# Layer 1's MLP: its norm's scale taken inside the first four chunks, their inputs split anew, and the residual turned without TensorE

## The chip, the cores and the metric

One NeuronCore of one Trainium2 chip runs the whole program. The metric is device time in microseconds (us), the median of several executions. Engines are named as the profile names them: PE is TensorE (PEld its weight loads), DVE is VectorE, ACT is ScalarE, POOL is GpSimd, SP is SyncE, which here only issues DMAs. Each engine works through its own queue of instructions in order; an instruction whose inputs are not there yet holds up all that stands behind it on the same engine.

## The reference, cut to what matters

512 tokens, 1024 channels, two layers. Layer 0 mixes by pooling, layer 1 by attention; each is followed by a gated MLP with a causal convolution of width 3 over the tokens.

```python
def rms_norm(x, g):
    return x * lax.rsqrt(jnp.mean(x * x, axis=-1, keepdims=True) + 1e-6) * g

def conv_glu_ffn(h, w_in, conv_w, conv_b, w_out):
    u = h @ w_in                                   # 512x1024 @ 1024x5632
    c = causal_depthwise_conv(u, conv_w) + conv_b  # 3 taps along the tokens
    a, g = c[..., :2816], c[..., 2816:]
    return (a * silu(g)) @ w_out                   # 2816 -> 1024

for i in range(2):
    h = h + mixer[i](rms_norm(h, norm_mix[i]))
    h = h + conv_glu_ffn(rms_norm(h, norm_ffn[i]), ...)
return rms_norm(h, norm_f)
```

The change is in the last MLP, that of layer 1.

## The kernel before, in words

**Arithmetic.** Every large product runs as three fast matmuls: an operand is split into a high part (a rounded copy, made by ACT) and a low part (the remainder, made by DVE), and `mm3` adds high x high (L89), high weight x low input (L90) and low weight x high input (L91) into one PSUM bank. A weight tile of 128x1024 thus costs one DMA from SP, one ACT copy (L103) and one DVE subtraction (L106). Three raw tiles, four high and four low tiles rotate.

**Layout.** Activations lie with channels on the partitions, `h[0..7]`, each 128x512 (two neighbours share one tile `hp[e]`). The inputs of the MLP, `f1x_h` and `f1x_l`, are the split of h times the norm's gain g; the norm's per-token factor r is not in them. At the end of attention, each `h[m]` gets its residual (L1232), is split (L244 makes `f1x_l`), and its squares are added to `n_acc`, by POOL (L220).

**Up-projection, `mlp_in`.** 44 chunks of 128 hidden channels, in the order gate 0, value 0, gate 1, value 1 and so on (`wi_0_1`, `wi_0_0`, `wi_1_1`, ...; the second number is 1 for the gate). A chunk is 8 k-steps of three matmuls, 24 matmuls into one bank. The first four chunks go together, k outermost: at each k, three matmuls for each of four banks. The bank ring is 5, 0, 1, 2, 3, 4. Call E the end of these 96 matmuls. Behind them comes the norm's statistics: a DVE reduction of `n_acc` (L225), a small matmul (L226), and 1/sqrt by three Newton steps in thirteen small DVE instructions (L186 to L200); ACT and DVE spread the result over all partitions as `n_rb` (L234, L236). Then, for each of the 44 chunks, `conv_chunk` multiplies the bank by `n_rb` into a buffer u (L681, DVE), ACT makes the first tap with the bias (L684), and DVE adds the other two (L685, L686). ACT applies silu to the gate (L724) and DVE multiplies (L733) and makes sums of halves for a later product with fewer multiplications (L738 to L761).

**Residual turned, `turned`.** The end of the kernel wants h with tokens on the partitions. PE transposes it by 32 matmuls with the identity (L792), eight sets of four into banks 6 and 7, and ACT copies each set out (L793, x8) into `ht`. A set is issued behind each of the eight chunks after the first group.

**Tokens and down-projection.** After 22 chunks, `mlp_tokens` multiplies by the down weights (`wt_...`, tiles a11, a12, a22 and their sums; some sums are formed by a second DMA that adds into the first one's tile, issued by POOL at L811), then the remaining chunks, another `mlp_tokens`, and an end part.

**Order.** A scheduler at build time orders each engine's instructions by its estimate of when they can run; `pin` keeps an instruction in the order of the source, and `tc.issue_after(x)` keeps what is inside behind x.

Of the kernel before, what the change touches and what calls it, by code (L numbers as in the profile page):

```python
# [37 lines left out]
NF = FF // P  # L38
# [24 lines left out]
def trunk(ctx: ExitStack, tc: tile.TileContext, x_tok, x_t, vecs, w_pool, w_kq, w_v, w_o, gain, w_in, w_half, w_down, w_end, w_tok, out):  # L63
    nc = tc.nc
    V, A, G, T = nc.vector, nc.scalar, nc.gpsimd, nc.tensor
# [46 lines left out]
    def in_weights(layer, j, s, eng=None, raw=None, pin=lambda ins: ins):  # L112
        return weights(w_in[layer][j, s], D, f"wi{layer}_{j}_{s}", eng, raw, 256 if eng else 1024, pin)

    pin = tc.keep_in_program_order
    eps = small(cst, 1, 32, name="eps")
    V.memset(eps, EPS)

    def load_root(x, name):

        A.activation(small(sm, 1, 32, tag="root", name=name), x, AF.Sqrt)

    load_root(eps, "root0")

# [30 lines left out]
    for g, w in enumerate(WINDOWS):  # L155
        b = band[:, g, :]
# [45 lines left out]
    class Norm:  # L202
# [5 lines left out]

        def square(self, c, lo, hi, sq=None):
            sq = sq or sm.tile([P, S], F32, tag="sq", name=f"{self.name}_sq{c}_{lo}")  # L210
            A.activation(sq[:, lo:hi], h[c][:, lo:hi], AF.Square)  # L211
# [19 lines left out]
        def spread(self, r):  # L231

            wide = sm.tile([P, S], F32, tag="sq", name=f"{self.name}_wide")
            A.activation(wide.rearrange("p (b i) -> p b i", i=SQ), r.unsqueeze(2).to_broadcast([P, NB, SQ]), AF.Copy)  # L234
            rb = sm.tile([P, S], F32, tag="rb", name=f"{self.name}_rb", bufs=1)
            V.transpose(rb, wide)  # L236
            return rb
# [124 lines left out]
    def mlp_halves(fp, xs, norm, ws0, after):  # L362
# [312 lines left out]
        for x in fills:  # L675
            pass

    def conv_chunk(fp, layer, ps, rb, m, name):

        u = fp.tile([P, S], F32, tag="u", name=f"{name}_u", bufs=3)  # L680
        V.tensor_tensor(u, ps, rb, ALU.mult)  # L681
        cw = [col(V_CW + (layer * 3 + t) * 2 * NF + m) for t in range(3)]
        t = fp.tile([P, S], F32, tag="t", name=f"{name}_t", bufs=4)
        A.activation(t, u, AF.Identity, bias=col(V_CB + layer * 2 * NF + m), scale=cw[2])  # L684
        V.scalar_tensor_tensor(t[:, 1:], u[:, : S - 1], cw[1], t[:, 1:], ALU.mult, ALU.add)  # L685
        V.scalar_tensor_tensor(t[:, 2:], u[:, : S - 2], cw[0], t[:, 2:], ALU.mult, ALU.add)  # L686
        return t

    def mlp_in(fp, layer, xs, norm, ws0, z, turns):

        pairs = [k for n, k in GROUPS for _ in range(n)]
        todo = [(j, s) for j in range(NF) for s in (1, 0)]
        together = 4 if ws0 is None else 2
        groups = [todo[i : i + together] for i in range(0, 4, together)] + [[t] for t in todo[4:]]
        conv, pend, r, rb, y = [None, None], [], None, None, None
        def load(group):
            return [ws0.pop(0) if ws0 else in_weights(layer, j, s) for j, s in group]

        stops, first = set(), 0
        for n, sums in GROUPS:  # L700
            first += 2 * n
            stops.add(min(first - 1 + sums, NF - 1))
        ahead = load(groups[0])
        for i, group in enumerate(groups):
            ws, ahead = ahead or load(group), None
            pss = [bank("ps") for j, s in group]
            for k in range(NC):
                for w, ps in zip(ws, pss):
                    mm3(ps, part(w, k), xs[k], k == 0, k == NC - 1)
# [4 lines left out]
            if rb is None:
                if len(pend) < 4:
                    continue
                if r is None:
                    r = norm.stats(bank("aux"))
                    continue
                rb = norm.spread(r)  # L720
            for (j, s), ps in pend:
                conv[s] = conv_chunk(fp, layer, ps, rb, s * NF + j, f"c{layer}_{j}_{s}")
                if s == 1:
                    A.activation(conv[1], conv[1], AF.Silu)  # L724
# [8 lines left out]
                V.tensor_tensor(o, conv[0], conv[1], ALU.mult)  # L733
                if pairs[e]:
                    if not odd:
                        split_sum(y, z[e], 0, 0, 1, -1.0 if layer else 1.0)
                    elif layer:
                        V.tensor_tensor(y[:, 4:6, :], y[:, 0:2, :], y[:, 1:4:2, :], ALU.subtract)  # L738
                        V.tensor_tensor(y[:, 6, :], y[:, 4, :], y[:, 3, :], ALU.add)
# [9 lines left out]
                if s == 0:  # L749
                    yield j  # L750
            pend = []
            next(turns, None)
# [17 lines left out]
    def mlp(fp, xs, norm):  # L770

        z, ht = [], []
        up = mlp_in(fp, 1, xs, norm, None, z, turned(fp, ht))
        done, first = 0, 0
        for g, (n, sums) in enumerate(GROUPS):
            upto = first + 2 * n
            while done < min(upto + sums, NF):
                done = next(up) + 1
            zg = z[first // 2 : upto // 2]
            if sums:  # L780
                mlp_tokens(g, zg, ht)
            first = upto
        return plain(zg), ht

    def turned(fp, ht):

        for j in range(NT):
            ht.append(fp.tile([P, D], F32, tag="ht", name=f"ht{j}", bufs=NT))
            for a in range(2):
                ps = bank("aux")  # L790
                for c in range(4):
                    T.transpose(ps[:, c * P : (c + 1) * P], h[4 * a + c][:, j * P : (j + 1) * P], ident)  # L792
# [173 lines left out]
    norm0, norm1, norm2 = (Norm(f"n{i}") for i in range(3))  # L966
# [7 lines left out]
    ws0 = []  # L974
# [7 lines left out]
    with tc.tile_pool(name="ap", bufs=2) as ap:  # L982
# [56 lines left out]
        for c in range(2):  # L1039
            u = ap.tile([P, S], F32, name=f"ku{c}", bufs=1)  # L1040
# [92 lines left out]
        todo = work()  # L1133
# [191 lines left out]
```

## Time and profile before

| | |
|---|---|
| median of 3 runs | 899.01 us (898.3 to 900.18) |
| profiled execution, its own time | 897.72 us |
| its span (first to last instruction) | 895.9 us |
| mean granted PE clock | 0.996 |
| busy: PE, PEld, DVE, ACT, POOL | 884.4, 765.6, 698.0, 475.6, 247.6 us |
| first group of four up chunks starts | 535.00 us |
| first token matmul | 637.02 us |

Times in the trace count from the start of the span. A row of the timeline gives start, length, engine, line, operation, output and inputs, a count, and in brackets how long the engine stood idle before it and what released it. A row of the groups gives the count, the busy sum and the mean of one in ns. Matmuls and DVE instructions overlap their neighbours, so their pace is the distance between starts, not their length.

### The profile page before, as it was taken

To read this page: it belongs to the slowest core of one execution; us is meant where nothing else is said; L and a number is where in the kernel's file an instruction comes from. 1 tells how busy PE (TensorE), PEld (TensorE's weight loads), DVE (VectorE), ACT (ScalarE), POOL (GpSimd) and SP (SyncE) were. 2 spreads that over 40 slices of the span, in tenths; PEclk is the share of its full clock that TensorE was granted. 3 is DMA by queue.
4 is the path that set the end of the run, shared out by engine and by line. 5 is a ranking of instruction groups with operands and counts; after the bars stand their busy time and mean duration, and the time that the engine had idled before them with its cause. 6 is when DMAs were issued, how large, how long until landed. Compare 5 with 4: busy or idle time off the path is not lost.

```text
span 895.9 us, 12904 instructions
## 1 busy us (share of the span) xinstructions
PE 884.4 (99%) x4770; PEld 765.6 (85%) x4770; DVE 698.0 (78%) x1110; ACT 475.6 (53%) x776; POOL 247.6 (28%) x327
## 2 busy tenths in 40 slices
PE   9999999999999999999999999999999999999996
PEld 8888889999999998898888888888888888888885
DVE  7899998878787876665887472999977888967744
ACT  7756655555464643546887451754534443434434
POOL 4867332313122300427665030001230002300004
PEclk9999999999999999999999999999999999999998
DMA  9444255565656443122110041175384231452202
GB/s 332 140 131 131 93 162 151 150 186 141 165 142 162 122 129 83 60 94 94 48 48 25 24 159 54 71 235 140 72 243 156 96 98 42 94 188 94 94 24 94
DMA packets 37118, 106.82 MB, mean 119 GB/s; under 512 B 3904, under 2 KB 5952, under 8 KB 37056
## 3 DMA queue, kind: packets, MB, share of 16 engines
q1 hardware_dynamic: 33600, 93.69, 31.8%
q0 software_dynamic: 3312, 12.06, 7.8%
q8 instruction: 37, 0.61, 0.3%
q10 hardware_dynamic: 144, 0.26, 0.1%
q14 instruction: 25, 0.20, 0.1%
HBM read 103.90 MB, written 2.10 MB: 118 GB/s over the span
## 4 chain that ended last, share of the span: by engine, by line
PE 89%; DVE 8%; ACT 1%; issue 1%; POOL 0%; ACTq 0%; DVEq 0%
PE bank L89 28%; PE bank L90 28%; PE bank L91 28%; PE bank L1157 1%; PE bank L1185 1%; DVE bank L393 1%; PE bank L288 1%; DVE tl L412 1%; DVE uw_hold_l L468 1%; PE bank L255 1%; DVE a_t L374 1%; ACT sc L1173 0%; DVE a_t L359 0%; DVE ty L420 0%; DVE g_t L358 0%
## 5 line engine op out<-in xcount | busy, mean ns | idle before, releaser
L89 PE MATMUL bank<-f1x_h,wi_h 128*128 128x512 f32 x352 | 137.7, 391 | 0.0
L90 PE MATMUL bank<-f1x_l,wi_h 128*128 128x512 f32 x352 | 137.0, 389 | 0.0
L91 PE MATMUL bank<-f1x_h,wi_l 128*128 128x512 f32 x352 | 136.8, 390 | 0.0
L103 ACT ACTIVATE wi_h<-wi_raw 128x1024 fp32r<-128x1024 f32 x58 | 61.3, 1060 | 86.5 <-PE bank L90 67.3
L91 PEld LDWEIGHTS bank<-f1x_h,wi_l 128*128 128x128 f32 x352 | 66.1, 188 | 13.9
L89 PEld LDWEIGHTS bank<-f1x_h,wi_h 128*128 128x128 f32 x352 | 66.1, 188 | 13.5
L90 PEld LDWEIGHTS bank<-f1x_l,wi_h 128*128 128x128 f32 x352 | 66.1, 188 | 13.5
L106 DVE TENSOR_TENSOR wi_l<-wi_raw,wi_h 128x1024 fp32r<-128x1024 f32 x44 | 53.8, 1225 | 27.0 <-ACT wi_h L103 27.0
L485 POOL TENSOR_TENSOR uw_r_raw<-uw_r_raw,uw_u_raw 128x512 f32<-128x512 f32 x15 | 25.0, 1668 | 161.7 <-DVE uw_hold_l L468 149.0
L106 POOL TENSOR_TENSOR wi_l<-wi_raw,wi_h 128x256 fp32r<-128x256 f32 x56 | 54.0, 994 | 27.3 <-ACT wi_h L103 27.3
L91 PE MATMUL bank<-th,uw_hold_l 128*128 128x256 f32 x180 | 50.9, 283 | 0.0
L90 PE MATMUL bank<-tl,uw_hold_h 128*128 128x256 f32 x180 | 50.9, 283 | 0.0
L89 PE MATMUL bank<-th,uw_hold_h 128*128 128x256 f32 x180 | 50.8, 282 | 0.0
L681 DVE TENSOR_TENSOR c_u<-bank,n_rb 128x512 f32<-128x512 f32 x44 | 30.1, 688 | 22.2 <-PE bank L91 22.0
L220 POOL TENSOR_TENSOR n_acc<-n_acc,n_sq 128x512 f32<-128x512 f32 x14 | 20.4, 1457 | 90.8 <-ACT n_sq L211 90.7
L90 PE MATMUL bank<-f0x_l,wi_h 128*128 128x512 f32 x112 | 43.6, 389 | 0.0
L91 PE MATMUL bank<-f0x_h,wi_l 128*128 128x512 f32 x112 | 43.6, 389 | 0.0
L89 PE MATMUL bank<-f0x_h,wi_h 128*128 128x512 f32 x112 | 43.0, 390 | 0.0
L531 DVE TENSOR_TENSOR h<-bank,h 128x512 f32<-128x512 f32 x48 | 32.9, 686 | 11.8 <-PE bank L91 11.4
L467 ACT ACTIVATE uw_hold_h<-wo_raw 128x512 fp32r<-128x512 f32 (+1 forms) x48 | 28.4, 591 | 25.7 <-PE bank L90 18.8
L686 DVE SCALAR_TENSOR_TENSOR c_t<-c_u,vec,c_t 128x510 f32<-128x510 f32 x44 | 40.9, 932 | 1.2
L823 POOL TENSOR_TENSOR wt_a_raw<-wt_a_raw,wt_s_raw 128x1024 f32<-128x1024 f32 x4 | 11.3, 2835 | 102.5 <-DVE wt_a_l L106 102.5
(437 smaller groups left out, 2771.6 us busy)
## 6 DMA issues: line engine op xcount, KB each, us to landing
wi_raw<-w_in SPq DMA_DIRECT2D x58, 512.0 KB, 3.3
wo_raw<-w_down SPq DMA_DIRECT2D x32, 256.0 KB, 2.7
uw_u_raw<-w_half SPq DMA_DIRECT2D x15, 512.0 KB, 5.5
uw_u_raw<-w_half POOLq DMA_DIRECT2D x15, 512.0 KB, 5.6
uw_r_raw<-w_half SPq DMA_DIRECT2D x15, 512.0 KB, 3.5
wt_a_raw<-w_tok SPq DMA_DIRECT2D x12, 512.0 KB, 3.8
kq_raw<-w_kq SPq DMA_DIRECT2D x10, 512.0 KB, 3.3
wo_raw<-w_o SPq DMA_DIRECT2D x8, 512.0 KB, 3.3
```

Source lines behind the costliest of these rows:

```text
L89: T.matmul(ps, lhsT=wh, rhs=xh, start=start, stop=False, **kw)
L90: T.matmul(ps, lhsT=wh, rhs=xl, start=False, stop=False, **kw)
L91: T.matmul(ps, lhsT=wl, rhs=xh, start=False, stop=stop, **kw)
L103: pin(A.activation(h[:, :n], raw[:, :n], AF.Copy))
L106: (eng or V).tensor_tensor(l[:, o], raw[:, o], h[:, o].bitcast(F32), ALU.subtract)
L220: eng.tensor_tensor(self.acc[:, lo:hi], self.acc[:, lo:hi], sq[:, lo:hi], ALU.add)
L467: A.activation(w[0], raw, AF.Copy)
L485: G.tensor_tensor(r[:, :n], r[:, :n], u[:, n:], ALU.add)
L531: V.tensor_tensor(h[m], ps, h[m], ALU.add)
L681: V.tensor_tensor(u, ps, rb, ALU.mult)
L686: V.scalar_tensor_tensor(t[:, 2:], u[:, : S - 2], cw[0], t[:, 2:], ALU.mult, ALU.add)
L823: G.tensor_tensor(r[:, :n], r[:, :n], raws["s1", s][:, :n], ALU.add)
```

## The change

Six edits, all around layer 1's MLP:

1. The statistics move into the first group, ahead of its third k-step, with 1/sqrt by ACT's square root (its table loaded during attention), a DVE reciprocal and one Newton step. The last addition into `n_acc` is DVE's instead of POOL's.
2. While the first group still runs, `rescale(k)` makes h times g times r for each of the eight inputs (DVE L708, into a buffer `xs_k`), then splits it anew into the same tiles: ACT L709 `f1x_h`, DVE L709 `f1x_l`. Both overwrite the inputs that the first group reads, so that each waits for the group's last matmul on that input.
3. The next chunk's weights (`wi_2_1`) are split between the fifth and the sixth of these, kept in the source's order.
4. Only the first four banks are still multiplied by `n_rb`, in place (L683), and not before the last rescaled input. The 40 later chunks go from PSUM straight to the taps (ACT L686, DVE L687, L688); their L681 is gone.
5. The next weights of the chunks after the first group are loaded as before in the source (`ahead = load(...)`).
6. The 32 PE transposes and eight ACT copies are gone. Four DVE transposes of 128x1024 (L813, within blocks of 32x32, all into one buffer `turn`) and 64 ACT copies of 32 partitions x 256 (L818) put h into `ht`: 16 copies beside the statistics, two behind each chunk's first tap, one behind each silu, the rest ahead of the tokens.

```diff
-        u = fp.tile([P, S], F32, tag="u", name=f"{name}_u", bufs=3)
-        V.tensor_tensor(u, ps, rb, ALU.mult)
+        if rb is not None:
+            V.tensor_tensor(ps, ps, rb, ALU.mult)
...
-        A.activation(t, u, AF.Identity, bias=col(V_CB + layer * 2 * NF + m), scale=cw[2])
...
+        taps.append(A.activation(t, ps, AF.Identity, bias=col(V_CB + layer * 2 * NF + m), scale=cw[2]))
+        V.scalar_tensor_tensor(t[:, 1:], ps[:, : S - 1], cw[1], t[:, 1:], ALU.mult, ALU.add)
+        V.scalar_tensor_tensor(t[:, 2:], ps[:, : S - 2], cw[0], t[:, 2:], ALU.mult, ALU.add)
...
+        def turn(n, ins):
+            with tc.issue_after(ins.ins):
+                for x in range(n):
+                    next(turns, None)
+
+        def rescale(k):
+            y = fp.tile([P, S], F32, tag="t", name=f"xs{layer}_{k}", bufs=4)
+            V.scalar_tensor_tensor(y, h[k], col(V_NFF + layer * NC + k), rb, ALU.mult, ALU.mult)
+            return pin(A.activation(xs[k][0], y, AF.Copy)), V.tensor_tensor(xs[k][1], y, xs[k][0].bitcast(F32), ALU.subtract)
...
             for k in range(NC):
+                if i == 0 and k == 2:
+                    r = norm.stats(bank("aux"), root=True)
+                    turn(12, norm.last)
+                    rb = norm.spread(r)
+                    turn(4, norm.wide)
                 for w, ps in zip(ws, pss):
                     mm3(ps, part(w, k), xs[k], k == 0, k == NC - 1)
...
+            if i == 0:
+                for k in range(NC):
+                    if k == 5:
+                        ahead = load(groups[1], pin)
+                    behind = rescale(k)
...
-            for (j, s), ps in pend:
-                conv[s] = conv_chunk(fp, layer, ps, rb, s * NF + j, f"c{layer}_{j}_{s}")
+            for (j, s), ps in zip(group, pss):
+                with ExitStack() as order:
+                    for x in () if i else behind:
+                        order.enter_context(tc.issue_after(x.ins))
+                    conv[s] = conv_chunk(fp, layer, ps, None if i else rb, s * NF + j, f"c{layer}_{j}_{s}")
+                if i:
+                    turn(2, taps[-1])
...
-                for c in range(4):
-                    T.transpose(ps[:, c * P : (c + 1) * P], h[4 * a + c][:, j * P : (j + 1) * P], ident)
-                A.activation(ht[j][:, a * S : (a + 1) * S], ps, AF.Copy)
...
+            V.transpose(x, hp[e])
...
+                    A.activation(
+                        whole[dst, :, 2 * e : 2 * e + 2, src].rearrange("p j c i -> p c j i"),
+                        x[src, :, :, q, :],
+                        AF.Copy,
+                    )
...
-            norm2.add(m)
+            norm2.add(m, eng=V if m == NC - 1 else G)
+            if m == NC // 2:
+                pin(load_root(eps, "root2"))
```

The instructions on DVE around the end of the first group. Before, this is the piece from the statistics' reduction on; the four `wi` splits are those of chunks 4, 5 and 6:

```order
L225 TENSOR_REDUCE n_part<-n_acc 128x16
L106 TENSOR_TENSOR wi_2_1_l<-wi_2_1_raw,wi_2_1_h 128x1024
L106 TENSOR_TENSOR wi_2_0_l<-wi_2_0_raw,wi_2_0_h 128x1024
L186 TENSOR_SCALAR rs_v<-bank_76 128x16
L106 TENSOR_TENSOR wi_3_1_l<-wi_3_1_raw,wi_3_1_h 128x1024
L188 TENSOR_SCALAR rs_i<-rs_v 128x16
```

The low part of chunk 6's weights, `wi_3_1_l`, is there the third split, ahead of the Newton steps and of everything that the convolutions do.

In the changed kernel the same queue goes from chunk 4's weights through the last rescaled inputs into the multiplications of the first four banks (bank 5 is `bank_75`, bank 0 `bank_70`):

```order
L106 TENSOR_TENSOR wi_2_1_l<-wi_2_1_raw,wi_2_1_h 128x1024
L709 TENSOR_TENSOR f1x_l<-xs_5_5801,f1x_h 128x512
L709 TENSOR_TENSOR f1x_l<-xs_6_5805,f1x_h 128x512
L106 TENSOR_TENSOR wi_2_0_l<-wi_2_0_raw,wi_2_0_h 128x1024
L709 TENSOR_TENSOR f1x_l<-xs_7_5809,f1x_h 128x512
L683 TENSOR_TENSOR bank_75<-bank_75,n_rb 128x512
L683 TENSOR_TENSOR bank_70<-bank_70,n_rb 128x512
L683 TENSOR_TENSOR bank_71<-bank_71,n_rb 128x512
L683 TENSOR_TENSOR bank_72<-bank_72,n_rb 128x512
L687 SCALAR_TENSOR_TENSOR c_0_1_t<-bank_75,vec,c_0_1_t 128x511
```

Six more tap instructions follow, on banks 5, 0, 1 and 2, and then this piece, on the first pair's products and chunk 4's taps (bank 3), which ends with the weights of chunk 6:

```order
L754 TENSOR_TENSOR y_0_5824<-c_0_0_t,c_0_1_t 128x512
L688 SCALAR_TENSOR_TENSOR c_1_0_t<-bank_72,vec,c_1_0_t 128x510
L779 SCALAR_TENSOR_TENSOR zl_0_5826<-y_0_5824,zh_0_5825 128x256
L754 TENSOR_TENSOR y_0_5824<-c_1_0_t,c_1_1_t 128x512
L687 SCALAR_TENSOR_TENSOR c_2_1_t<-bank_73,vec,c_2_1_t 128x511
L759 TENSOR_TENSOR y_0_5824<-y_0_5824 128x512
L688 SCALAR_TENSOR_TENSOR c_2_1_t<-bank_73,vec,c_2_1_t 128x510
L760 TENSOR_TENSOR y_0_5824<-y_0_5824 128x256
L106 TENSOR_TENSOR wi_3_1_l<-wi_3_1_raw,wi_3_1_h 128x1024
L761 TENSOR_TENSOR y_0_5824<-y_0_5824 128x256
```

`wi_3_1_l` is still the third split, but no longer right behind the second: the last rescaled input, the four banks, their taps and the first products have moved ahead of it. From `wi_2_1_l` to it, both counted, there are now 25.

On PE, before, at the start of chunk 6 (bank 5 for the second time), two transposes of a set stand ahead of its plain rows of three:

```order
L792 MATMUL bank_76<-ident,h_98 128x128 x2
L792 MATMUL bank_76<-ident,h_99 128x128 x2
L89 MATMUL bank_75<-f1x_h,wi_3_1_h 128x512
L90 MATMUL bank_75<-f1x_l,wi_3_1_h 128x512
L91 MATMUL bank_75<-f1x_h,wi_3_1_l 128x512
L89 MATMUL bank_75<-f1x_h,wi_3_1_h 128x512
```

In the changed kernel, at the same place:

```order
L91 MATMUL bank_74<-f1x_h,wi_2_0_l 128x512
L89 MATMUL bank_75<-f1x_h,wi_3_1_h 128x512
L90 MATMUL bank_75<-f1x_l,wi_3_1_h 128x512
L89 MATMUL bank_70<-f1x_h,wi_3_0_h 128x512
L90 MATMUL bank_70<-f1x_l,wi_3_0_h 128x512
L89 MATMUL bank_71<-f1x_h,wi_4_1_h 128x512
L90 MATMUL bank_71<-f1x_l,wi_4_1_h 128x512
L91 MATMUL bank_75<-f1x_h,wi_3_1_l 128x512
L89 MATMUL bank_75<-f1x_h,wi_3_1_h 128x512
```

The transposes are gone, and the first two matmuls of chunks 7 and 8 have moved ahead of chunk 6's first use of `wi_3_1_l`.

On SP, the DMAs ahead of the first token stage (`wt_0` and `wt_1` are its two sets of weights; a `wt_s` tile gets its second half from POOL's adding DMA, and its sum with the `a` tile is one more weight). Before:

```order
L95 DMA wi_8_0_raw<-w_in 128x1024
L817 DMA wt_1_a_raw<-w_tok 128x1024
L810 DMA wt_1_s_raw<-w_tok 128x1024
L817 DMA wt_0_a_raw<-w_tok 128x1024
L817 DMA wt_1_a_raw<-w_tok 128x1024
L817 DMA wt_0_a_raw<-w_tok 128x1024
L810 DMA wt_0_s_raw<-w_tok 128x1024
```

In the changed kernel:

```order
L95 DMA wi_8_0_raw<-w_in 128x1024
L846 DMA wt_1_a_raw<-w_tok 128x1024
L846 DMA wt_0_a_raw<-w_tok 128x1024
L846 DMA wt_1_a_raw<-w_tok 128x1024
L846 DMA wt_0_a_raw<-w_tok 128x1024
L839 DMA wt_1_s_raw<-w_tok 128x1024
L839 DMA wt_0_s_raw<-w_tok 128x1024
```

The first `wt_1_s` has moved behind three `wt_a` transfers, and now waits for the split of the first `wt_0_s` on DVE, where before it waited for a matmul only.

More of the change, by code (lines that the diff above doesn't have):

```diff
@@ L119, in load_root @@
     def load_root(x, name):
-        A.activation(small(sm, 1, 32, tag="root", name=name), x, AF.Sqrt)
+        return A.activation(small(sm, 1, 32, tag="root", name=name), x, AF.Sqrt)
     load_root(eps, "root0")
@@ L210, in square @@
             sq = sq or sm.tile([P, S], F32, tag="sq", name=f"{self.name}_sq{c}_{lo}")
-            A.activation(sq[:, lo:hi], h[c][:, lo:hi], AF.Square)
+            self.last = A.activation(sq[:, lo:hi], h[c][:, lo:hi], AF.Square)
             return sq
@@ L233, in spread @@
             wide = sm.tile([P, S], F32, tag="sq", name=f"{self.name}_wide")
-            A.activation(wide.rearrange("p (b i) -> p b i", i=SQ), r.unsqueeze(2).to_broadcast([P, NB, SQ]), AF.Copy)
+            self.wide = A.activation(wide.rearrange("p (b i) -> p b i", i=SQ), r.unsqueeze(2).to_broadcast([P, NB, SQ]), AF.Copy)
             rb = sm.tile([P, S], F32, tag="rb", name=f"{self.name}_rb", bufs=1)
@@ L676, in mlp_halves, with mlp_in, load @@
             pass
+    taps = []
     def conv_chunk(fp, layer, ps, rb, m, name):
-        u = fp.tile([P, S], F32, tag="u", name=f"{name}_u", bufs=3)
-        V.tensor_tensor(u, ps, rb, ALU.mult)
+        if rb is not None:
+            V.tensor_tensor(ps, ps, rb, ALU.mult)
         cw = [col(V_CW + (layer * 3 + t) * 2 * NF + m) for t in range(3)]
         t = fp.tile([P, S], F32, tag="t", name=f"{name}_t", bufs=4)
-        A.activation(t, u, AF.Identity, bias=col(V_CB + layer * 2 * NF + m), scale=cw[2])
-        V.scalar_tensor_tensor(t[:, 1:], u[:, : S - 1], cw[1], t[:, 1:], ALU.mult, ALU.add)
-        V.scalar_tensor_tensor(t[:, 2:], u[:, : S - 2], cw[0], t[:, 2:], ALU.mult, ALU.add)
+        taps.append(A.activation(t, ps, AF.Identity, bias=col(V_CB + layer * 2 * NF + m), scale=cw[2]))
+        V.scalar_tensor_tensor(t[:, 1:], ps[:, : S - 1], cw[1], t[:, 1:], ALU.mult, ALU.add)
+        V.scalar_tensor_tensor(t[:, 2:], ps[:, : S - 2], cw[0], t[:, 2:], ALU.mult, ALU.add)
         return t
-    def mlp_in(fp, layer, xs, norm, ws0, z, turns):
+    def mlp_in(fp, layer, xs, norm, z, turns):
         pairs = [k for n, k in GROUPS for _ in range(n)]
         todo = [(j, s) for j in range(NF) for s in (1, 0)]
[L693 to L697, printed above, removed]
+        groups = [todo[:4]] + [[t] for t in todo[4:]]
+        conv = [None, None]
+        def load(group, *more):
+            return [in_weights(layer, j, s, None, None, *more) for j, s in group]
+        def turn(n, ins):
[6 more added lines that the diff above has]
+            return pin(A.activation(xs[k][0], y, AF.Copy)), V.tensor_tensor(xs[k][1], y, xs[k][0].bitcast(F32), ALU.subtract)
         stops, first = set(), 0
@@ L707, in mlp_in @@
             for k in range(NC):
+                if i == 0 and k == 2:
[3 more added lines that the diff above has]
+                    turn(4, norm.wide)
                 for w, ps in zip(ws, pss):
                     mm3(ps, part(w, k), xs[k], k == 0, k == NC - 1)
-            pend += zip(group, pss)
+            if i == 0:
[3 more added lines that the diff above has]
+                    behind = rescale(k)
             j, s = group[-1]
-            if s == 1 or j not in stops:
+            if i and (s == 1 or j not in stops):
                 ahead = load(groups[i + 1])
[L714 to L720, printed above, removed]
-            for (j, s), ps in pend:
-                conv[s] = conv_chunk(fp, layer, ps, rb, s * NF + j, f"c{layer}_{j}_{s}")
+            for (j, s), ps in zip(group, pss):
[5 more added lines that the diff above has]
+                    turn(2, taps[-1])
                 if s == 1:
-                    A.activation(conv[1], conv[1], AF.Silu)
+                    silu = A.activation(conv[1], conv[1], AF.Silu)
+                    if i:
+                        turn(1, silu)
                     continue
@@ L748, in mlp_in @@
                     split_sum(y, z[e], 2 * odd, 2 * odd, 2)
[L749 to L752, printed above, removed]
+                yield j
     def split_sum(y, z, i, o, n, sign=1.0):
@@ L772, in mlp @@
         z, ht = [], []
-        up = mlp_in(fp, 1, xs, norm, None, z, turned(fp, ht))
+        turns = turned(fp, ht)
+        up = mlp_in(fp, 1, xs, norm, z, turns)
         done, first = 0, 0
@@ L779, in mlp @@
             zg = z[first // 2 : upto // 2]
+            for x in turns:
+                pass
             if sums:
@@ L785, in turned @@
     def turned(fp, ht):
[L787 to L790, printed above, removed]
-                for c in range(4):
-                    T.transpose(ps[:, c * P : (c + 1) * P], h[4 * a + c][:, j * P : (j + 1) * P], ident)
-                A.activation(ht[j][:, a * S : (a + 1) * S], ps, AF.Copy)
-                yield
+        whole = fp.tile([P, NT, NC, P], F32, name="ht", bufs=1)
+        ht.extend(whole[:, j].rearrange("p c i -> p (c i)") for j in range(NT))
+        G4 = P // SQ
+        for e in range(NC // 2):
+            x = fp.tile([P, 2 * S], F32, tag="turn", name=f"turn{e}", bufs=1)
+            V.transpose(x, hp[e])
+            x = x.rearrange("p (c j q i) -> p c j q i", c=2, j=NT, q=G4)
+            for g in range(G4):
+                for q in range(G4):
+                    src, dst = slice(g * SQ, (g + 1) * SQ), slice(q * SQ, (q + 1) * SQ)
+                    A.activation(
[3 more added lines that the diff above has]
+                    )
+                    yield
     def mlp_tokens(g, z, ht):
```

## The prediction

> **What bounds the kernel now.** I read the page's busy times and chain of waits first, then what PE waited for.
>
> ```profile
> span 895.9 us, 12904 instructions
> PE 884.4 (99%) x4770; PEld 765.6 (85%) x4770; DVE 698.0 (78%) x1110; ACT 475.6 (53%) x776; POOL 247.6 (28%) x327
> PE 89%; DVE 8%; ACT 1%; issue 1%; POOL 0%; ACTq 0%; DVEq 0%
> PE bank L255 <- DVE warm L253: 2.2, 1, 2.2
> PE bank L89 <- DVE h L531: 0.6, 1, 0.6
> ```
>
> PE is busy for 99% of the span, the chain runs on it, and its only listed waits are 2.2 us at the start and 0.6 us in layer 0. So time is won only by taking work from PE, and lost wherever PE now waits; nothing makes such a wait up later, because PE has no slack behind it. DVE's 78% is an average: what counts is whether its queue delivers in order what PE needs next.
>
> PE's timeline gives the pace and the places. The two token rows are 55 triples apart: 37.40/55 = 0.680 us a triple, 0.2267 a matmul, 5.44 a chunk of 24.
>
> ```profile
> 535.00 0.39 PE L89 MATMUL bank<-f1x_h,wi_h 128*128 128x512 f32 x1
> 556.76 0.29 PE L226 MATMUL bank<-n_part,groups 128*128 128x16 f32 x2
> 562.22 0.39 PE L91 MATMUL bank<-f1x_h,wi_l 128*128 128x512 f32 x1
> 562.45 0.60 PE L792 MATMUL bank<-ident,h 128*128 128x128 f32 x4
> 563.35 0.40 PE L91 MATMUL bank<-f1x_h,wi_l 128*128 128x512 f32 x1
> 637.02 0.39 PE L89 MATMUL bank<-wt_a_h,zh 128*128 128x512 f32 x1
> 674.42 0.39 PE L89 MATMUL bank<-wt_a_h,zh 128*128 128x512 f32 x1
> ```
>
> E, the end of the first group, is 556.76; T, the first token matmul, 637.02. Between 535.00 and T lie 18 chunks: 432 x 0.2267 = 97.9 of the 102.0 us. The other 4.1 are the statistics' matmul, the transposes and one short wait.
>
> **The transposes, what is won.** One set of four costs PE 563.35 - 562.22 - 0.680 = 0.45 us. Eight sets are 3.6; the 4.1 above less 0.3 for L226, which only moves, allow 3.8 at most. I take **-3.7**. DVE's 40 multiplications that go too (L681, 0.69 us each) free no PE time.
>
> **DVE's queue behind the first group, what is lost.** Here is the term that decides: the low part of chunk 6's weights, `wi_3_1_l`. Rows of DVE's and ACT's timeline, then DVE groups that price the queue:
>
> ```profile
> 555.78 2.36 DVE L106 TENSOR_TENSOR wi_l<-wi_raw,wi_h 128x1024 fp32r<-128x1024 f32 x2 [15.94 <-ACT wi_h L103]
> 558.15 1.21 DVE L106 TENSOR_TENSOR wi_l<-wi_raw,wi_h 128x1024 fp32r<-128x1024 f32 x1
> 559.28 0.17 DVE L188 TENSOR_SCALAR rs_i<-rs_v 128x16 int32<-128x16 int32 x1
> 567.29 1.28 ACT L724 ACT_TABLE_LOAD   x1 [0.99 <-DVE c_t L686]
> L681 DVE TENSOR_TENSOR c_u<-bank,n_rb 128x512 f32<-128x512 f32 x44 | 30.1, 688 | 22.2 <-PE bank L91 22.0
> L685 DVE SCALAR_TENSOR_TENSOR c_t<-c_u,vec,c_t 128x511 f32<-128x511 f32 x44 | 32.7, 746 | 0.0
> L739 DVE TENSOR_TENSOR y<-y 128x256 f32<-128x256 f32 x8 | 3.4, 423 | 0.2
> ```
>
> Before, chunk 4's low weights start at 555.78 = E - 0.98, when the group releases their buffers, and `wi_3_1_l` is done at 559.36, long before chunk 6. In the changed order 24 instructions run from `wi_2_1_l` on before it is its turn. Starts lie 0.08 us less than a length apart (558.15 + 1.21 against 559.28), so:
>
> - two weight splits (`wi_2_1_l`, `wi_2_0_l`), 2 x 1.14 = 2.3
> - ten 512-wide two-input operations (three L709, four L683, two L754, one L759), 10 x 0.61 = 6.1
> - ten taps, 10 x 0.67 = 6.7
> - two of 256, 2 x 0.34 = 0.7
> - `wi_3_1_l` itself, 1.2
>
> Together 17.0, so that it is done at E + 16.0 if nothing holds DVE up. PE needs it after chunks 4 and 5 (48 matmuls) and the six that the scheduler put ahead: E + 54 x 0.2267 = E + 12.2. PE waits at least 3.8. On top come DVE's own waits in that stretch: for ACT's first tap of `c_0_1` (ACT has a weight copy ahead of it that waits for a DMA), and for silu behind the table load of 1.28. I put 0.6 on them, between 0 and 1.8: **+4.4**, from 3.6 (DVE's lengths 1% shorter) to 5.6 (the DMA ahead of that copy late by a microsecond more). One wait only: behind it the splits of chunks 7 and 8 follow within 2 to 5 us, ahead of their need.
>
> **The clock, a consequence of that wait.** The tail shows what PE's clock does without matmuls; the columns are the stretch, its length, then busy times and counts, the clock, and the DMAs.
>
> ```profile
> 887.03 0.39 PE L91 MATMUL bank<-we_h,zl 128*128 128x512 f32 x1
> 888.00:889.00 1.00, 0.00 (x0) 0.00 (x0) 0.86 (x5) 0.78 (x3) 0.00 (x0) 1.00 0.00 0
> 889.00:890.00 1.00, 0.00 (x0) 0.00 (x0) 0.77 (x6) 0.87 (x3) 0.00 (x0) 0.70 0.04 16
> 890.00:891.00 1.00, 0.00 (x0) 0.00 (x0) 0.67 (x1) 0.70 (x1) 0.00 (x0) 0.50 0.91 352
> ```
>
> The last matmul ends at 887.42; the mean of 0.70 puts the fall to half at about 889.4, 2.0 us later. A wait of 4.4 us is longer than that. The waits listed above are too short to show a fall and a return, and no row tells how long the clock stays down once matmuls run again; if it returns as fast as it falls, 2.0 us at half speed cost **+1.0**. The ends are 0 (no fall) and 2.2 (at half speed for as long as the wait itself).
>
> The Trainium skill ("TensorE: Matmul & The Clock Gate", Part 1, What's actually happening) has the clock fall after an idle window of about 3.4 us and return after a busy one of about 3.4 us; it speaks against this change. The trace agrees that the clock halves without matmuls, though 2.0 us after the last one. By the page's window the price, an estimate, would be 1.7 and the sum 0.7 higher.
>
> **The statistics in the group.** The last addition of squares moves from POOL to DVE, ahead of the reduction:
>
> ```profile
> 536.07 1.22 DVE L106 TENSOR_TENSOR wi_l<-wi_raw,wi_h 128x1024 fp32r<-128x1024 f32 x1 [0.18 <-ACT wi_h L103]
> 537.31 1.79 POOL L220 TENSOR_TENSOR n_acc<-n_acc,n_sq 128x512 f32<-128x512 f32 x1 [3.65 <-ACT n_sq L211]
> 539.13 0.71 DVE L225 TRANSPOSE_TENSOR_REDUCE n_part<-n_acc 128x16 f32<-128x512 f32 x1 [1.18 <-POOL n_acc L220]
> ```
>
> POOL's 1.79 become DVE's 0.7, so the sum is ready sooner, and PE's third k-step, at 535.00 + 24 x 0.2267 = 540.4, finds it. But DVE's transpose of the first residual pair now stands ahead of the low part of the fourth chunk's weights, which PE may then reach a little early: **+0.1**, between 0 and 0.4.
>
> **The rescaled inputs.** Eight L708 and eight L709 are 16 x 0.65 = 10.4 us on DVE; the wait of 15.94 us ahead of 555.78 covers all L708 and the first splits. Those of inputs 5 to 7 are in the 17.0 above. PE needs the last at chunk 4's eighth k-step, E + 21 x 0.2267 = E + 4.8; DVE has it out by E - 0.98 + 2.3 + 3 x 0.61 = E + 3.2. Cost 0, with 1.6 us to spare.
>
> **The turning copies.** ACT has no copy of 32 x 256; the nearest row is a tap stage's 128 x 256, 0.41 us, 0.31 from start to start. 64 of them are 20 us, on an engine that is 53% busy and idle for 17.5 us ahead of E:
>
> ```profile
> 554.69 2.96 ACT L103 ACTIVATE wi_h<-wi_raw 128x1024 fp32r<-128x1024 f32 x3 [17.52 <-PE bank L90]
> L757 ACT ACTIVATE zh<-y 128x256 fp32r<-128x256 f32 x8 | 3.3, 412 | 10.9 <-DVE y L733 10.9
> 562.61 0.70 DVE L236 STREAM_TRANSPOSE n_rb<-n_wide 128x512 f32<-128x512 f32 x1
> ```
>
> The first 16 (5 us) lie in that pause: 0. Four DVE transposes of 128x1024, twice the row's width, are some 1.3 us each; one lies in DVE's own pause of 15.94, the others beside chunks that have lost two L681 each: 0. Two behind a tap cost ACT 0.6 a chunk of 5.44: 0. If a copy takes twice that, ACT still has room, but the 17.0 us queue above waits longer, up to 1 us more: this is in the 5.6.
>
> **The token stage.** The last 16 copies stand on ACT ahead of the token weights, and `wt_1_s` is fetched later:
>
> ```profile
> 604.70 0.42 SPq L810 DMA_DIRECT2D wt_s_raw<-w_tok  x1
> 635.74 1.22 DVE L106 TENSOR_TENSOR wt_s_l<-wt_s_raw,wt_s_h 128x1024 fp32r<-128x1024 f32 x1
> 637.02 5.18 SPq L810 DMA_DIRECT2D wt_s_raw<-w_tok  x2
> 641.37 0.88 POOL L811 DMA_DIRECT2D wt_s_raw<-w_tok  x1 [9.07 <-DMA wt_s_raw<-w_tok]
> 629.47 2.84 POOL L823 TENSOR_TENSOR wt_a_raw<-wt_a_raw,wt_s_raw 128x1024 f32<-128x1024 f32 x1 [3.56 <-DVE wt_a_l L106]
> 630.09 2.77 DVE L686 SCALAR_TENSOR_TENSOR c_t<-c_u,vec,c_t 128x510 f32<-128x510 f32 x1
> ```
>
> It went out at T - 32; now it waits for the split of `wt_0_s`, which ended at T - 0.1 and ends about 2 us sooner where POOL's second addition is gone from its way (beside that addition a tap took 2.77 us instead of 0.75). Issue at T - 2.5, landing 4.35 later (637.02 to 641.37), the adding DMA as long again plus 1.5: T + 7.7, its copy 1.06: T + 8.8. PE needs it after 36 matmuls, at T + 8.2. Late by 0.6, and the sixteen copies or POOL's addition, which now falls beside the splits, can add 2. I take **+0.8**, between 0 and 3.
>
> **The sum.** -3.7 + 4.4 + 0.1 + 0.8 = +1.6, and +1.0 with the clock: +2.6. The profiled execution of 897.72 us would become 900.3; it is 1.3 below the median 899.01, on which the forecast stands: 901.6.
>
> **The rivals.**
> A. The wait comes, the clock does not fall: +1.6, 900.6, from 899.5 to 902. For it: the wait may be nearer 3.6, and the tail is one case only. Against it: 2.0 us were enough there.
> B. The forecast, wait and clock: 901.6, from 900.6 to 904.
> C. Faster: `wi_3_1_l` comes in time, because ACT or the group's release lets DVE run earlier than these rows say; only the transposes count, with 0.9 for the small terms: -2.8, 896.2, from 895.2 to 897.2. Its point: DVE would have to be 3.8 us ahead, which the release at E - 0.98 forbids unless the 24 instructions ahead run a fifth shorter. That the new order does nothing is in it: the transposes leave PE in any case.
> D. The token stage is late in its whole chain of sums, not once: its DMAs run some 6 us later, and the last of it and the next chunk's weights lose their margin of 1 to 2 us: 2 to 3 us more than B, 904.
>
> **Chances.** B 0.46, A 0.26, C 0.15, D 0.13. What this measurement can tell from no change is 0.2%, 1.8 us: 897.2 to 900.8. Faster is C, 0.15. Within it lie A's lower half and B's lower edge, 0.13 and 0.08. The rest, 0.64, is slower. The range from 896.8 to 904.2 leaves out most of C and half of D. B's own is 900.6 to 904.
>
> **What would show it.** PE's waits list one for the low part of `wi_3_1` (L91 behind DVE L106) of 3.6 to 5.6 us, near E + 12; the clock in the slices behind it is under 1; no L792; from the first up chunk to the first token matmul 102 - 3.7 + 4.4 + 1.0 us. Wrong would be no such wait, or a second of its size elsewhere: at the rescaled inputs, or at `wt_1_s`.

## The result, and the profile after

The changed kernel takes 904.3 us, median of six runs (902.4 to 907.2), against 898.6 before: 1.0064 of it, 95% interval 1.0042 to 1.0087. It is slower, by 5.7 us where 2.6 had been forecast. The profiled execution took 903.0 us. The page of the changed kernel:

```profile
span 901.2 us, 12896 instructions
PE 883.3 (98%) x4738; PEld 763.4 (85%) x4738; DVE 678.3 (75%) x1083; ACT 502.9 (56%) x843; POOL 241.6 (27%) x326
PE 85%; DVE 10%; ACT 3%; issue 1%; DMA 0%; POOL 0%; ACTq 0%; DVEq 0%
```

What PE waited for in it, beside the two waits of before and one of 0.3 us at the start of layer 0 (us in total, times, longest):

```profile
PE bank L91 <- DVE wi_l L106: 5.6, 1, 5.6
PE bank L89 <- ACT wt_s_h L103: 1.8, 2, 1.6
```

32 matmuls fewer, and two new waits: one for the low part of an up weight, one for a weight of the token stage. The timeline of PE shows the first at chunk 6's low weights, and what follows it:

```profile
535.51 0.39 PE L89 MATMUL bank<-f1x_h,wi_h 128*128 128x512 f32 x1
569.64 0.39 PE L90 MATMUL bank<-f1x_l,wi_h 128*128 128x512 f32 x1
575.65 0.79 PE L91 MATMUL bank<-f1x_h,wi_l 128*128 128x512 f32 x1 [5.62 <-DVE wi_l L106]
576.24 0.63 PE L89 MATMUL bank<-f1x_h,wi_h 128*128 128x512 f32 x1
578.80 0.46 PE L89 MATMUL bank<-f1x_h,wi_h 128*128 128x512 f32 x1
579.11 0.40 PE L90 MATMUL bank<-f1x_l,wi_h 128*128 128x512 f32 x1
641.26 0.39 PE L89 MATMUL bank<-wt_a_h,zh 128*128 128x512 f32 x1
651.21 0.73 PE L89 MATMUL bank<-wt_s_h,zh 128*128 128x512 f32 x2 [1.62 <-ACT wt_s_h L103]
681.77 0.39 PE L89 MATMUL bank<-f1x_h,wi_h 128*128 128x512 f32 x1
893.70 0.39 PE L91 MATMUL bank<-we_h,zl 128*128 128x512 f32 x1
```

Between 569.64 and 575.65 PE loses 6.01 - 0.23 = 5.8 us. From 576.24 to 578.80 six matmuls take 0.43 us each instead of 0.227; with the two at the ends that is 1.6 us more. The clock's column (the third from the end) in windows of that stretch says why:

```profile
571.00:572.00 1.00, 0.00 (x0) 0.00 (x0) 1.00 (x3) 1.00 (x3) 0.00 (x0) 1.00 0.00 0
572.00:572.25 0.25, 0.00 (x0) 0.00 (x0) 0.25 (x2) 0.24 (x2) 0.00 (x0) 0.74 0.00 0
572.25:578.50 6.25, 2.85 (x7) 2.27 (x8) 6.25 (x9) 4.35 (x7) 0.00 (x0) 0.50 0.25 84
578.50:579.00 0.50, 0.50 (x3) 0.40 (x2) 0.50 (x1) 0.05 (x1) 0.00 (x0) 0.55 0.90 180
```

It fell to half at 572.1 (a mean of 0.74 over the 0.25 us from 572.00) and returned at 578.95 (a mean of 0.55 over the half us from 578.50), 3.3 us after PE had work again.

By stages, on PE: from the first up chunk to the first token matmul 641.26 - 535.51 = 105.8 us, 3.7 more than before (+5.8 wait, +1.6 clock, -3.7 transposes); from there to chunk 18 (the `f1x_h` row at 681.77) 40.5 us against 38.1, +2.4, of which 1.8 are listed waits and the rest the wider spacing of the matmuls around them; from there to PE's last matmul 211.93 us in both. That is +6.1. The span grew by 5.3 only: the first up chunk began 0.5 us later, and the tail behind PE was 1.4 us shorter, to which the eighth experiment comes back. The 0.5 are not shown to be the change's: in that experiment, whose code up to there is that of the kernel before, the chunk began 0.8 us later.

### The profile page after: what moved, and what is told of

It reads as the page before. It is cut to its first block, busy times and chain, and to the rows that moved or that the text cites. A ratio compares the mean times of both kernels' runs of the same rounds, so it can differ in the third digit from the quotient of the medians.

```text
span 901.2 us, 12896 instructions
## 1 busy us (share of the span) xinstructions
PE 883.3 (98%) x4738; PEld 763.4 (85%) x4738; DVE 678.3 (75%) x1083; ACT 502.9 (56%) x843; POOL 241.6 (27%) x326
## 4 chain that ended last, share of the span: by engine, by line
PE 85%; DVE 10%; ACT 3%; issue 1%; DMA 0%; POOL 0%; ACTq 0%; DVEq 0%
PE bank L89 27%; PE bank L91 27%; PE bank L90 27%; PE bank L1186 1%; PE bank L1214 1%; DVE bank L393 1%; PE bank L288 1%; DVE tl L412 1%; ACT ht L818 1%; DVE uw_hold_l L468 1%; DVE a_t L374 0%; ACT sc L1202 0%; DVE a_t L359 0%; DVE g_t L358 0%; DVE ty L420 0%
## 5 line engine op out<-in xcount | busy, mean ns | idle before, releaser
L90 PE MATMUL bank<-f0x_l,wi_h 128*128 128x512 f32 x112 | 43.6, 389 | 0.0
L91 PE MATMUL bank<-f0x_h,wi_l 128*128 128x512 f32 x112 | 43.6, 389 | 0.0
L468 DVE TENSOR_TENSOR uw_hold_l<-wo_raw,uw_hold_h 128x512 fp32r<-128x512 f32 (+1 forms) x48 | 36.6, 762 | 1.4 <-ACT uw_hold_h L467 1.4
L1202 ACT ACTIVATE sc<-sc,neg 128x257 f32<-128x257 f32 (+1 forms) x64 | 30.3, 476 | 10.6 <-DVE neg L1189 10.0
```

The lines of the kernel that those rows point to most:

```text
L90: T.matmul(ps, lhsT=wh, rhs=xl, start=False, stop=False, **kw)
L91: T.matmul(ps, lhsT=wl, rhs=xh, start=False, stop=stop, **kw)
L468: V.tensor_tensor(w[1], raw, w[0].bitcast(F32), ALU.subtract)
L1202: A.activation(t, t, AF.Exp, bias=neg[:, i : i + 1], scale=-1.0, accum_out=den[:, i : i + 1])
```

## The experiments

The kernel before was run beside each of them; its medians lay between 898.6 and 898.9. Below, "to the tokens" is the time from the first up chunk to the first token matmul (102.0 us before, 105.8 after), "token stage" the time from there to chunk 18 (38.1 and 40.5).

**1. The order of DVE's queue.** Chunk 5's and 6's weights are loaded right behind the last rescaled input, ahead of the first convolutions.

```diff
                     behind = rescale(k)
+                queue += [load(groups[2]), load(groups[3])]
...
             if i and (s == 1 or j not in stops):
-                ahead = load(groups[i + 1])
+                if i > 2:
+                    queue.append(load(groups[i + 1]))
```

> The changed kernel with the weights of chunks 5 and 6 loaded and split right behind the last rescaled input, ahead of the first four convolutions (chunk 7 again one chunk ahead). Theory (DVE's order makes the wait): PE's wait for wi_3_1's low part, 5.6 us and 5.8 with its neighbours, and the 1.6 us of half clock behind it go, no other wait takes their place: 904.3 - 7.4 = 896.9, between 896 and 898.5. Rival (ACT, loaded with turning copies and with weight copies that wait for DMAs, is what is late): a wait of 2 us or more moves to chunk 7 or 8, 900 to 902. The token wait of 2.4 stays by both.

Measured 897.7 us, 0.9992 of the kernel before (0.9982 to 1.0001). The wait for `wi_l` is gone, to the tokens it takes 98.3 us, and no wait moved to chunk 7 or 8. So the order was the cause; the edit moves the DMA and ACT's copy along with the split, but an ACT that is overloaded by itself would have shown a wait at chunk 7 or 8, and that rival falls. (What ACT adds to the length is the fourth experiment's.) The total is 0.8 us over the expected 896.9, because the token stage took 42.2 us instead of 40.5. Its waits are the same two as in the changed kernel, to 0.01 us, as PE's timeline shows:

```profile
644.26 0.73 PE L89 MATMUL bank<-wt_s_h,zh 128*128 128x512 f32 x2 [1.62 <-ACT wt_s_h L103]
645.21 0.74 PE L89 MATMUL bank<-wt_s_h,zh 128*128 128x512 f32 x2 [0.22 <-ACT wt_s_h L103]
```

But here the clock fell behind them, as the windows show:

```profile
642.00:645.75 3.75, 1.91 (x7) 0.78 (x5) 1.51 (x2) 3.70 (x6) 3.16 (x2) 1.00 0.00 0
646.25:649.50 3.25, 3.25 (x9) 2.52 (x8) 2.42 (x3) 0.80 (x1) 0.00 (x0) 0.50 0.96 149
649.50:650.00 0.50, 0.50 (x4) 0.40 (x3) 0.05 (x1) 0.05 (x1) 0.00 (x0) 0.98 0.92 295
```

With equal waits, the difference of the two stages, 42.2 - 40.5 = 1.7 us, is the price of one fall. Why equal waits had unequal ends is told in the last section.

**2. The token stage.** Three copies behind each tap instead of two.

```diff
-                    turn(2, taps[-1])
+                    turn(3, taps[-1])
```

> The changed kernel with three turning copies behind each chunk's tap instead of two, so that the fourth residual pair is turned some ten chunks earlier. Theory (late turning holds the token stage up: its buffer and the copies ahead of the weight copies on ACT): the token waits, 2.4 us in PE's pace, go; the wait at chunk 6 stays within 5.5 to 6.2: 904.3 - 2.4 = 901.9, 901 to 903. Rival (the later adding DMA is late for reasons of its own, such as bandwidth): token waits of 1.5 or more stay, 903.5 to 905.

Measured 903.0 us (902.0 to 903.5), 1.0046 of before (1.0031 to 1.0061). The token stage is back at 38.1 us, and its waits are gone; the late turning was their cause, in two ways that this run does not separate. In the changed kernel the copies stood on ACT ahead of the weight copy, and the sum's data were there at 649.1, when POOL's addition starts. ACT's timeline:

```profile
646.67 3.40 ACT L818 ACTIVATE ht<-turn 32x256 f32<-32x256 f32 x8
650.10 1.06 ACT L103 ACTIVATE wt_s_h<-wt_s_raw 128x1024 fp32r<-128x1024 f32 x1
```

POOL's:

```profile
649.13 2.35 POOL L852 TENSOR_TENSOR wt_a_raw<-wt_a_raw,wt_s_raw 128x1024 f32<-128x1024 f32 x1 [5.70 <-DMA wt_s_raw<-w_tok]
```

With three copies a chunk no such row of eight stands there, and the first of the sums' DMAs that was at T - 3.1 is issued at T - 18. But the wait at chunk 6 was 6.9 us in the profiled execution instead of the expected 5.5 to 6.2, and the half clock behind it cost 0.8 us more than in the changed kernel; to the tokens it takes 107.8 us, which took back 2 of the 2.4 us there. The longer wait goes back to a DMA, as the fourth experiment shows.

**3. Filling the gap.** 20 matmuls of 128x512 into an unused bank ahead of chunk 6.

```diff
+                if i == 3 and k == 0:
+                    spare = bank("aux")
+                    for x in range(20):
+                        T.matmul(spare, lhsT=part(ws[0], x % NC)[0], rhs=xs[x % NC][0], start=x == 0, stop=x == 20 - 1)
```

> The changed kernel with 20 spare matmuls of 128x512 into an unused bank ahead of chunk 6, 4.5 us of PE work inside the wait. Theory (the clock falls because PE idles about 2.2 us): PE's wait shrinks to about 1.1 us, the clock stays at 1.00 there, and the 1.6 us go: 904.3 - 1.6 = 902.7, 902 to 903.5. Rival (the clock falls for another reason, or the spare work delays DVE or chunk 6): clock 0.5 for about 3 us behind the wait as before, or a longer wait; 904 to 906.

Measured 904.9 us (904.2 to 905.9), 1.0069 (1.0052 to 1.0086). The expectation missed. The low weights came 0.5 us later still (40.7 us behind the first up chunk against 40.1), so that 1.9 us of wait remained, and those were enough for the clock to fall. PE's timeline, then the windows:

```profile
577.04 0.65 PE L91 MATMUL bank<-f1x_h,wi_l 128*128 128x512 f32 x1 [1.85 <-DVE wi_l L106]
```

```profile
577.00:577.25 0.25, 0.21 (x1) 0.21 (x2) 0.25 (x2) 0.00 (x0) 0.00 (x0) 0.97 0.00 0
577.25:580.50 3.25, 3.25 (x9) 2.47 (x9) 3.25 (x4) 1.48 (x1) 0.00 (x0) 0.50 0.57 192
```

It shows that about 1.9 us without matmuls can suffice, less than the 2.2 that I had assumed. That the clock can be kept by filling, this run does not show; the sixth has a gap that was filled.

**4. The length of the wait.** ACT's copy of chunk 8's weights behind the first silu (`silus` collects them).

```diff
-                ahead = load(groups[i + 1])
+                with ExitStack() as order:
+                    if i == 4:
+                        order.enter_context(tc.issue_after(silus[0].ins))
+                    ahead = load(groups[i + 1])
```

> The changed kernel with ACT's copy of chunk 8's weights (wi_4_1) put behind the first silu instead of ahead of it. Theory (beside DVE's queue of 17 us, the wait at chunk 6 holds 1.5 to 2 us in which DVE waits for silu, which stands on ACT behind a copy that waits for its DMA): the wait falls from 5.6 to 3.6 to 4.3, the clock still falls: 904.3 - 1.6 = 902.7, 902 to 903.8. Rival (DVE's queue alone, or the turning copies, make the length): the wait stays at 5.3 or more, 904 to 905.

The wait fell from 5.6 to 3.2 us, more than expected, and to the tokens it takes 103.4 us, 2.4 less. So DVE's own wait for silu, 2.1 us, was the second part of the length; the rest of the 2.4 is the split's place, one short instruction (L760, 0.3 us) further ahead. Of the changed kernel, ACT's timeline, then DVE's:

```profile
566.89 1.06 ACT L103 ACTIVATE wi_h<-wi_raw 128x1024 fp32r<-128x1024 f32 x1 [1.83 <-DMA wi_raw<-w_in]
567.97 1.28 ACT L743 ACT_TABLE_LOAD   x1
```

```profile
569.93 0.69 DVE L754 TENSOR_TENSOR y<-c_t,c_t 128x512 f32<-128x512 f32 x1 [2.14 <-ACT c_t L743]
574.38 1.22 DVE L106 TENSOR_TENSOR wi_l<-wi_raw,wi_h 128x1024 fp32r<-128x1024 f32 x1
```

The copy of `wi_4_1` waits 1.83 us for its DMA and holds the table load and silu behind it, DVE waits 2.14 for silu, and PE for DVE. In the second experiment's trace the same DMA made ACT wait 2.9 us, and PE 6.9; in the third's 2.6 us, and the low weights came 0.5 later: this chain hands a late transfer on to PE. That fits the spread of the changed kernel's runs, 4.8 us, against 1.9 before. The clock has a part in this spread, too: its mean was 0.996 in the fastest run and 0.992 in the slowest. Which of the two weighs more is not shown.

The total, though, was 904.6 us (1.0069, 1.0053 to 1.0086), above the expected 902 to 903.8: what was won was given back. The token stage took 43.6 us: from the adding DMA's issue on POOL to the addition that waits for it were 8.0 us instead of 6.6, and the clock fell a second time. PE's waits:

```profile
PE bank L91 <- DVE wi_l L106: 3.2, 1, 3.2
PE bank L89 <- ACT wt_s_h L103: 2.3, 2, 2.1
PE bank L90 <- DVE wt_s_l L106: 0.8, 1, 0.8
```

**5. Both waits mended.** As in 1 and 2, and chunks up to 14 get their weights two chunks ahead.

```diff
+                queue += [load(groups[2]), load(groups[3])]
...
-            if i and (s == 1 or j not in stops):
-                ahead = load(groups[i + 1])
...
+            while i and i < 16 and len(queue) < 1 + (i < 12) and i + len(queue) < end:
+                queue.append(load(groups[i + 1 + len(queue)]))
...
-                    turn(2, taps[-1])
+                    turn(3, taps[-1])
```

> Both waits taken away together: the weights of chunks 5 and 6 split ahead of the first convolutions, from chunk 4 to 14 weights two chunks ahead, and three turning copies behind each tap. Theory (the changed kernel loses by these two waits and the clock's falls behind them, and by nothing else): from the first up chunk to the first token matmul 98.3 us against 102.0 before, the token stage 38.1 as before, clock 1.00 throughout: 898.7 - 3.7 = 895.0, 894.3 to 896. Rival (more work for ACT and DMAs that come in other places give part back wherever PE is early): a new wait of 1 us or more, with or without a fall of the clock, 896.5 to 899.

Measured 893.4 us (893.3 to 894.2), 0.9942 of before (0.9928 to 0.9955): better than both kernels. To the tokens 98.25 us, token stage 38.08, no wait in layer 1's MLP, and the clock at 9 in every slice:

```profile
span 891.5 us, 12898 instructions
PE 881.4 (99%) x4738; PEld 763.3 (86%) x4738; DVE 681.8 (76%) x1083; ACT 503.5 (56%) x843; POOL 244.2 (27%) x326
PEclk9999999999999999999999999999999999999999
```

From the first up chunk to PE's last matmul it needs 348.3 us against 352.0 before. These 3.8 us are the transposes, whole. Another 1.4 are the tail's; the expectation left them out, and so lies 0.9 to 2.6 us too high.

**6 and 7. Each half alone.** In the sixth, PE turns the residual as before (`next(turns, None)` issues one set of four transposes), and the rest is the changed kernel:

```diff
-                if i:
-                    turn(2, taps[-1])
...
+                    if i:
+                        next(turns, None)
```

> The changed kernel with the residual turned by PE again (32 transposes, ACT copies of 128x512), one set behind each chunk: the scale's part alone. Theory: DVE's queue of 17 us delays wi_3_1's low part as before, but transposes that stand ready fill part of PE's wait, so that no idle stretch is over 1.5 us and the clock stays: wait of 2 to 3.5 us in pieces, the token stage 38.1: 898.7 + 1.5 to 3 = 900.2 to 901.7. Rival (the wait is made by the turning copies on ACT): no wait at chunk 6, 898.7 or less.

898.2 us, 0.9995 (0.9986 to 1.0004): no difference, and 2 us below the expected 900.2, of which the tail has 1.4. The number is the rival's, 898.7 or less; its mechanism is not. On PE it is 1.0 us slower than before, all of it ahead of the tokens. The scheduler put transposes into the gap, as PE's timeline shows:

```profile
572.55 1.11 PE L811 MATMUL bank<-ident,h 128*128 128x128 f32 x8
573.86 1.15 PE L811 MATMUL bank<-ident,h 128*128 128x128 f32 x8 [0.20 <-ACT ht L812]
575.36 0.44 PE L811 MATMUL bank<-ident,h 128*128 128x128 f32 x2 [0.35 <-ACT ht L812]
575.55 0.48 PE L91 MATMUL bank<-f1x_h,wi_l 128*128 128x512 f32 x1
```

Chunk 6's low weights (575.55) come 38.7 us behind the first up chunk, against 40.1 in the changed kernel. PE without transposes would use them at 34.4 (569.64 + 0.23 - 535.51 in the changed kernel), so 4.3 of the 5.8 us of delay are there with no turning copy on ACT at all, against the rival. But PE's listed waits in it are 0.5 us in all, and the clock stays. Taking the transposes from PE thus also took away what would have filled this gap.

In the seventh, DVE and ACT turn the residual, five copies behind each chunk's tap, in the kernel before; its bank is multiplied in place, so that the taps read it as in the changed kernel.

> The kernel before with the residual turned by DVE and ACT, five copies behind each chunk's tap; the bank is multiplied by the scale in place, since the buffer of the products has to make room. Theory: 3.7 us of PE work go, but DVE, which still multiplies all 44 banks, loses 5 us to transposes where before it was just in time for chunks 8 to 10, and gives 2 to 4.5 us back in waits for low weights there: 897 to 900. Rival (the turned part is a gain on any ground): 895 to 896, no wait over 0.5.

899.8 us, 1.0011 (1.0002 to 1.0020). PE waits 3.3 us for low weights, 1.0 in the first group and 2.3 at chunk 9 with a fall of the clock behind it; from the first up chunk to its last matmul it needs 2.3 us more than before. So the 3.7 us of the transposes were no gain where DVE still multiplies all banks; with the other half, which takes 40 of these multiplications from DVE, they are (fifth experiment).

**8. The tail.** The kernel before with 24 tiny ACT copies of a constant.

```diff
+                for x in range(3):
+                    A.activation(small(sm, 1, 32, tag="root", name=...), eps, AF.Copy)
```

> The kernel before with 24 tiny ACT copies (128x1, of a constant) added, three behind each copy of a turned set: nothing else changes. In every kernel measured so far but the one before, the last output DMA's issue on ACT takes 0.37 us and the run ends 7.0 us behind PE's last matmul; in the one before it takes 2.36 and 8.5. Theory (the 2.36 hang on where that instruction lies in ACT's stream, which any other number of ACT instructions moves): 0.37 and 7.0 here too, 898.7 - 1.4 = 897.3. Rival (they belong to something that the change and its halves each removed): 2.36 and 8.5 as before, 898.7 to 899.

897.4 us, 0.9987 (0.9979 to 0.9996), as expected. The last output DMA's issue on ACT, before:

```profile
890.73 2.36 ACTq L941 DMA_DIRECT2D out<-o  x1
```

And in this kernel:

```profile
891.58 0.37 ACTq L943 DMA_DIRECT2D out<-o  x1
```

So 1.2 to 1.4 us of every comparison with the kernel before here come from how many ACT instructions stand ahead of that one, not from what the change does: against such a padded kernel before, the changed one loses 6.9 us, and the better version wins 4.0. The trace before also holds a candidate for the reason. In the 2.5 us from 890.7, which are the long issue, its DMA queues show a load of instructions (queue and kind, packets, MB, share of the engines):

```profile
q14 instruction: 1, 0.01, 0.8%
```

In the other ten traces no load on that queue falls into the last issue on ACT, and it takes 0.37 us; in the padded kernel the load comes 11.7 us sooner (879.9 instead of 891.6). That one delays the other fits, but no run tested it.

**9. One chunk ahead.** The fifth without its second chunk of lead, which is the edits of the first and the second together.

> Both waits mended as in the better version, but the weights only one chunk ahead, as in the changed kernel. Theory (with DVE's queue in this order, chunk 9's low weights wi_4_0 come behind the taps and sums of the chunks ahead): one wait of 0.5 to 2 us at chunk 9, with a fall of the clock (1.7) if it reaches about 1.5: 893.4 + 0.5 to 3.7 = 893.9 to 897. Rival (two chunks ahead changes nothing): no wait, 893.4.

895.6 us, 0.9966 (0.9953 to 0.9978). Two waits, 1.3 us in all, the longer 1.1, without a fall of the clock; the second chunk of lead is worth about 2 us.

## Why the prediction was wrong

It named the right waits and the right sign, and its sum was too small by 3 us. Three of its terms failed by size: DVE's own waits (0.6 assumed, 2.1 measured), the clock's return (2.0 us assumed, 3.3 measured) and the token stage (0.8 assumed, 2.4 measured, the largest miss).

- **Transposes, -3.7:** right, 3.8 in the fifth experiment.
- **Chunk 6's low weights, +4.4:** mechanism and place right, the size was 5.8. The queue's 17.0 us were right: from 556.63 to 575.60 are 19.0, less the 2.1 us in which DVE waited for silu 16.8. The term that was mis-sized is "0.6 for DVE's own waits", which I had put between 0 and 1.8. I had looked at the weight copy ahead of the first tap; a second one, for chunk 8, stands ahead of silu and waits for its DMA. The group's end also released DVE 0.2 us later than assumed, but PE came to the place 0.3 later, too.
- **The clock, +1.0:** it fell, as in case B; the size was 1.6. The step "if it returns as fast as it falls" failed: PE worked 3.3 us at half clock, not 2.0. By the window of 3.4 us of the Trainium skill ("TensorE: Matmul & The Clock Gate", What's actually happening) the estimate was 1.7, and the first experiment measured 1.7.
- **The token stage, +0.8:** 2.4, within the stated 0 to 3. Two of its numbers were off: a turning copy takes 0.42 us from start to start, not 0.31 (eight in 3.40), and the sum's data were there 7.9 us behind T (649.13 - 641.26, forecast 7.7), but ACT, with eight copies still ahead, took them up 1.0 us later. So the first weight was late by 1.8 us instead of 0.6, and the matmuls behind it lost 0.6 more.
- **Statistics, +0.1:** no wait there.
- **Rescaled inputs at no cost:** right; PE waits for none.
- **Not foreseen:** the tail's -1.4. The issue of 2.36 us stood in the profile before, but nothing there said that it would shrink.

Together -3.7 + 5.8 + 1.6 + 2.4 - 1.4 = +4.7 us, and with the start's 0.5 the 5.3 of the span to 0.1. The medians differ by 5.7; the changed kernel's runs lie up to 4.8 us apart (fourth experiment). The forecast of 901.6 and its upper end of 904.2 were too low, since B's wait was longer than its row sum and the token stage cost three times its term. It did so once and not in its whole chain as in case D, whose 904 is near the result by coincidence.

## What to carry to other kernels

Where PE has no slack, read for each weight how many instructions stand ahead of its split in DVE's queue, and what each of those waits for on other engines: a queue of 17 us was counted right and still was late by another 2, through a copy that waited for a DMA on a third engine. Work that is taken from PE is a gain only if PE then has other work ready; keep the idle stretch that is left short, because a fall of the clock adds 1.7 us: here stretches of 1.1 us never had one behind them, one of 1.6 us had one in one run and none in two others, and in this MLP those of 1.9 us and more each had one. And when a change moves the number of instructions, compare PE's stages, not only the totals: a microsecond can come from the tail.

## What the runs showed of the hardware

- **The clock changes on a fixed grid of 3.41 us.** Half-clock spells ahead of the tail were 3.4 or 6.8 us long: 646.1 to 649.5 in the first experiment, 577.2 to 580.6 in the third, 572.1 to 578.95 after. The first began 1.8 us after PE had resumed work. In the clock's records of the six traces where it fell more than once (after, experiments 1 to 4, 7), any two changes lie a whole number of 3.413 us apart, up to 95 of them (572.12 and 896.39 after).
- **What counts is how much of one such window is idle.** The first two rows are windows of the first experiment, the other two of the changed kernel, with the same wait of 1.62 us:

```profile
642.69:646.10 3.41, 1.63 (x5) 0.89 (x6) 1.86 (x2) 3.37 (x6) 2.75 (x2) 1.00 0.00 0
646.10:649.52 3.42, 3.42 (x10) 2.67 (x9) 2.57 (x3) 0.95 (x2) 0.00 (x0) 0.50 0.99 150
647.22:650.63 3.41, 2.36 (x11) 1.63 (x9) 1.08 (x2) 3.32 (x8) 1.50 (x1) 1.00 0.19 36
650.63:654.05 3.42, 2.63 (x10) 1.81 (x11) 2.87 (x3) 3.37 (x4) 1.67 (x2) 1.00 0.35 34
```

In the first experiment 1.78 us of one window are idle, and the next runs at half clock. In the changed kernel the wait lies across a boundary, 1.05 us in one window and 0.79 in the next, and the clock stays. In the third experiment the same wait lies across a boundary, too (1.07 and 0.77), and the clock stays. So it was luck that this wait cost the changed kernel no second fall.

The sharp bound is open. In the fourth experiment a window with 1.75 us idle (646.03 to 649.45) kept the clock, and the next, with 1.33, was followed by half clock. An estimate from all eleven traces, from 110 us on: if a window is counted as ending 0.4 us ahead of the recorded change, and a 128x512 matmul as 0.227 us, its pace, then every window at full clock that was followed by half clock had at least 1.75 us idle, about half of it, and every other at most 1.68.

The Trainium skill ("TensorE: Matmul & The Clock Gate", What's actually happening) states a free-running window of 3413 ns, and the traces agree. It also states that the clock falls after at least one idle window; here 1.78 us of one window were enough.

- **The issue of the last DMA on ACT takes 0.37 or 2.36 us;** 24 ACT instructions more ahead of it made the difference. A load of instructions inside the long one (eighth experiment) may be why.
